# Four gated levels as products with only the second halves' queries, in a RetNet and HGRN2 step on one core

## The chip, the core and the metric

The kernel runs on one NeuronCore of a Trainium2 chip. Its time is the device time of one execution in microseconds (us), the median of several runs. TensorE (PE in the profile) multiplies matrices. It first loads a stationary operand (LDWEIGHTS, listed as the engine PEld) and then streams a moving operand past it (MATMUL). VectorE (DVE), ScalarE (ACT) and GpSimd (POOL) work element by element on 128 partitions. SyncE (SP) issues the DMA transfers. Products land in PSUM, everything else lies in SBUF.

## The reference, cut to what matters

One decoder layer is run for a prompt of 2048 tokens and for eight samples of 8 tokens each. After a norm and one input projection there are four RetNet heads and four HGRN2 heads. The change is in the HGRN2 heads, which are a linear recurrence with a forget gate of its own for every feature:

```
b = jnp.cumsum(gb, axis=2)
diff = b[:, :, :, None, :] - b[:, :, None, :, :]
decay = jnp.exp(jnp.where(causal[:, :, None], diff, -jnp.inf))
A = jnp.einsum('bhtd,bhsd,bhtsd->bhts', qb, kb, decay)
o = jnp.einsum('bhts,bhsv->bhtv', A, vb) + jnp.einsum('bhtd,bhdv->bhtv', qb * jnp.exp(b), S)
```

`A[t, s]` is needed for all pairs s <= t within a chunk. Its decay depends on the feature d, so it is not one product of queries and keys. A head norm, a gate, the output projection and a squared-ReLU MLP follow.

## The kernel before

Tokens are worked on in three groups of 640, 768 and 704 (the last with the 64 sample tokens ahead of 640 of the prompt). For each group `mix` runs four heads, and one call of `mixer` does a RetNet and an HGRN2 head together on chunks of 128 tokens. A group has 5, 6 and 5 chunks, in two segments: 2 and 3, 3 and 3, 2 and 3. So there are 12 calls of `mixer`, with 64 chunks in all. After the mixing come the output projection and the MLP (`ffn`) of the three groups, which the change does not touch.

Projections are written as three float32r products each (high part by high part, high by low, low by high). They are the matmuls of L344, L751 and L1212, and they fill PE. The work of a head is laid between them: `mixer` enters its steps into an agenda at given ticks, a tick being one step of a projection (six matmuls), and a scheduler then orders each engine's instructions.

The matrix `A` of a chunk (tile `AT`, transposed: keys by queries; `ATs` for the samples) is put together from levels. On the level of w in `LEVELS = (64, 32, 16, 8, 4, 2)` a chunk falls into blocks of 2w tokens, and the pairs are those with the key in the first half of a block and the query in its second half. `exponents`, `decays` and `decayed` make a tile `qk` that holds decayed keys in first halves and decayed queries in second halves, so that the features can be summed by a product.

- For w = 64 and 32 `corners` (L978) multiplies each first half by its second half: 64 by 64 or 32 by 32 columns.
- For w = 16, 8 and 4 `kept` (L921, for the samples L915) multiplies the whole chunk by itself, 128 by 128 columns in float32, and `copy_predicated` (L922, L916) copies the entries of this level's mask `msk[:, i]` into `AT`.
- For w = 2, blocks of four tokens, `quad_products` (L989) forms the four products of a block's two keys and two queries feature by feature on DVE, `quad_parts` cuts them into two float32r parts (ACT L351, DVE L352), and `quad` sums over features by `column_sums`, two matmuls with a matrix of ones as stationary operand (L512, L513). Copies of 64 elements (L1010, L1008) place the four results.
- Neighbours (w = 1) and the diagonal have steps of their own, also with `column_sums`.

A float32 matmul is listed as two passes, each with its own LDWEIGHTS. `mm` gives PSUM tiles out of four buffers, and `pj` is a pool of two for the projections. A projection's result leaves PSUM by `normed` (DVE L650). Where a row names L853, these are the transposes of `turn`; L784 and L787 are the sample outputs, L798 the cutting of sample values, L1069 the decayed keys of the chunk's end.

Of the kernel before, what the change touches and what calls it, by code (L numbers as in the profile page):

```python
# [13 lines left out]
ALU = mybir.AluOpType  # L14

P = 128
# [4 lines left out]
SLEN = 8  # L21
NS = NSEQ * SLEN
# [11 lines left out]
LEVELS = (64, 32, 16, 8, 4, 2)  # L34
NLV = len(LEVELS) + 2
# [67 lines left out]
def in_groups(sample, prompt):  # L103

    out = []
    for ns, p0, n in GROUPS:
        out += [sample[:ns], prompt[p0:p0 + n]]
    return np.concatenate(out, 0)


def constants():
    c = np.zeros((P, NCONST), np.float64)
    c[:, C_ID:C_ID + P] = np.eye(P)
    s = np.arange(P)[:, None]
    t = np.arange(P)[None, :]
    sc = DK ** -0.5
    same = (s // SLEN == t // SLEN) & (s < NS) & (t < NS)
    for h, g in enumerate(GAM):
        dec = np.where(s <= t, g ** np.maximum(t - s, 0), 0.0) * sc
        c[:, C_RM + h * P:C_RM + (h + 1) * P] = dec  # L120
        c[:, C_RS + h * P:C_RS + (h + 1) * P] = np.where(same, dec, 0.0)
        c[:, C_GQ + h * P:C_GQ + (h + 1) * P] = g ** (t + 1.0)
        c[:, C_GS + h * NS:C_GS + (h + 1) * NS] = g ** (np.arange(NS) % SLEN + 1.0)
        c[:, C_KS + h] = sc * g ** (P - 1.0 - s[:, 0])
        c[:, C_KSS + h] = sc * g ** (SLEN - 1.0 - s[:, 0] % SLEN)
    c[:, C_SM:C_SM + 4] = (s % 32 // SLEN == np.arange(4)[None, :])
    m = np.zeros((P, 2 * NLV, P), np.float32)
    for i, w in enumerate(LEVELS + (1,)):
        lv = (s // (2 * w) == t // (2 * w)) & (s % (2 * w) < w) & (t % (2 * w) >= w)
        m[:, i] = lv  # L130
        m[:, NLV + i] = lv & (s < NS) & (t < NS) & (w < SLEN)

    i = LEVELS.index(2)
    m[:, 0], m[:, NLV] = m[:, i] * (s % 2), m[:, NLV + i] * (s % 2)
    m[:, NLV - 1] = s == t
    m[:, 2 * NLV - 1] = (s == t) & (s < NS)
    half = DK // 2
    inv = np.power(10000.0, (-np.arange(half, dtype=np.float32) / np.float32(half)).astype(np.float64)).astype(np.float32)
    pos = in_groups(np.tile(PAST + np.arange(SLEN), NSEQ), np.arange(SEQ)).astype(np.float32)
    ang = (inv[:, None] * pos[None, :]).astype(np.float64)  # L140
    cs = np.zeros((P, 2, NT), np.float32)
    cs[:half, 0] = cs[half:, 0] = np.cos(ang)
    cs[:half, 1] = -np.sin(ang)
    cs[half:, 1] = np.sin(ang)
    return c.astype(np.float32), m.astype(np.uint8).reshape(P, -1), cs.reshape(P, -1)
# [57 lines left out]
class Kernel:  # L203
# [5 lines left out]
    def at(self, when, fn, *a):  # L209
        heapq.heappush(self.agenda, (when, self.n_at, fn, a))  # L210
        self.n_at += 1
# [651 lines left out]
    def mixer(self, g, p, b, t0):  # L863


        nc, T, n0 = self.nc, g.T, g.ns
        con, msk = self.con, self.msk
        n = g.n // C
        q, k, f = b["q"], b["k"], b["f"]
        rq, rk = b["rq"], b["rk"]  # L870
        cols = [slice(n0 + C * c, n0 + C * (c + 1)) for c in range(n)]
        x = {}
        at = lambda t, fn, *a: self.at(t0 + t, fn, *a)
# [15 lines left out]
        def blocks(t, w, a):  # L889
            return t[:, a:T].rearrange("p (n h m) -> p n h m", h=2, m=w)  # L890
# [13 lines left out]
        def decayed(w):  # L904
            a = 0 if w < SLEN else n0
            qk = x["qk", w] = self.get()
            D4, Q4 = blocks(x["dd", w], w, a), blocks(qk, w, a)
            nc.vector.tensor_tensor(out=Q4[:, :, 0, :], in0=D4[:, :, 0, :], in1=blocks(k, w, a)[:, :, 0, :], op=ALU.mult)
            nc.vector.tensor_tensor(out=Q4[:, :, 1, :], in0=D4[:, :, 1, :], in1=blocks(q, w, a)[:, :, 1, :], op=ALU.mult)

        def kept(i, qk, sg):

            if sg == 2:
                ps = self.mm(P)
                nc.tensor.matmul(ps, qk[:, :P], qk[:, :P], start=True, stop=True)  # L915
                nc.vector.copy_predicated(self.ATs, msk[:, NLV + i], ps)  # L916
                return
            seg, m = g.segs[sg], len(g.segs[sg])
            ps = self.mm(m * P)
            for j, c in enumerate(seg):  # L920
                nc.tensor.matmul(ps[:, j * P:(j + 1) * P], qk[:, cols[c]], qk[:, cols[c]], start=True, stop=True)  # L921
            nc.vector.copy_predicated(self.AT[sg][:, :m], msk[:, i].unsqueeze(1).to_broadcast([P, m, P]),  # L922
                                      ps.rearrange("p (c t) -> p c t", t=P))


        def own_products():
# [42 lines left out]
        def corners(w, sg):  # L969

            nb = P // (2 * w)
            seg, m = g.segs[sg], len(g.segs[sg])
            qk = x["qk", w]
            ps = self.mm(m * nb * w)
            for j, c in enumerate(seg):
                for r in range(nb):
                    s0 = cols[c].start + 2 * w * r
                    nc.tensor.matmul(ps[0:w, (r * m + j) * w:(r * m + j + 1) * w], qk[:, s0:s0 + w], qk[:, s0 + w:s0 + 2 * w],  # L978
                                     start=True, stop=True)
            for r in range(nb):  # L980
                nc.scalar.copy(self.AT[sg][2 * w * r:2 * w * r + w, :m, 2 * w * r + w:2 * w * (r + 1)],
                               ps[0:w, r * m * w:(r + 1) * m * w].rearrange("p (c t) -> p c t", t=w))


        def quad_products():
            x["quad"] = self.get()
            Q4 = x["qk", 2][:, :T].rearrange("p (n h m) -> p n h m", h=2, m=2)
            shape = [P, T // 4, 2, 2]
            nc.vector.tensor_tensor(out=x["quad"][:, :T].rearrange("p (n i j) -> p n i j", i=2, j=2),  # L989
                                    in0=Q4[:, :, 1].unsqueeze(3).to_broadcast(shape),  # L990
                                    in1=Q4[:, :, 0].unsqueeze(2).to_broadcast(shape), op=ALU.mult)

        def quad_parts():
            x["quad_hi"], x["quad_lo"] = self.getr(), self.getr()
            self.cut(x["quad"], x["quad_hi"], x["quad_lo"], T, 3)

        def quad(sg):
            seg, m = g.segs[sg], len(g.segs[sg])
            a, e = self.seg_cols(g, seg)
            s0 = cols[seg[0]].start  # L1000
            second = lambda t: t.rearrange("p (n h i) -> p n h i", h=2, i=2)[:, :, 1]
            ps = self.mm(e - a)
            self.column_sums(ps, x["quad_hi"][:, a:e], x["quad_lo"][:, a:e])
            p4 = ps.rearrange("p (n i j) -> p n i j", i=2, j=2)
            nb, nq = (s0 - a) // 4, P // 4
            for j, i in ((0, LEVELS.index(2)), (1, 0)):
                if nb:
                    nc.vector.copy_predicated(second(self.ATs[:, :NS]), second(msk[:, NLV + i, :NS]), p4[:, :nb, :, j])  # L1008
                for c in range(m):
                    nc.vector.copy_predicated(second(self.AT[sg][:, c]), second(msk[:, i]),  # L1010
                                              p4[:, nb + c * nq:nb + (c + 1) * nq, :, j])

        def level(i, sg):
            w = LEVELS[i]
            if w == 2:
                quad(sg)
            elif w >= 32:
                corners(w, sg)
            else:
                kept(i, x["qk", w], sg)  # L1020
# [99 lines left out]
            x["gate", i, hd] = self.gate_norm(g, x["po", i][hd], a, e, b["gh" if hd else "gr"], self.eps_h if hd else self.eps, g.o[p][hd])  # L1120

        parts = range(3 if n0 else 2)
        step, late, chunk, wait = 13, 24, 7, 14
        at(0, logs)
        at(4, scans)
        at(40, own_products)
# [7 lines left out]
        for i, w in enumerate(LEVELS):  # L1134
            t = 6 + step * i
            at(t, exponents, w)
            at(t + 8, decays, w)
            at(t + 11, decayed, w)
            if w == 2:
                at(t + 16, quad_products)  # L1140
                at(t + 20, quad_parts)
            for sg in (parts if 2 < w < SLEN else range(2)):
                at(t + late + 3 * sg + (wait if w == 2 else 9 if w >= 32 else 4), level, i, sg)
        for sg in parts:
            at(46 + 4 * sg, ret_scores, sg)
            at(60 + 4 * sg, turn, "ktr", rk, sg, C_KS)
# [1 line left out]
        t = 6 + step * len(LEVELS)  # L1148
# [680 lines left out]
```

## Time and profile before

| | us |
|---|---|
| median of 3 runs (2497.9 to 2498.38) | 2497.9 |
| the profiled execution | 2499.3 |
| its span, first to last instruction | 2497.5 |
| PE busy, share of the span | 2483.4 (99%) |
| PEld busy | 2465.2 (99%) |
| DVE busy | 1883.1 (75%) |
| ACT busy | 1246.5 (50%) |
| POOL busy | 371.2 (15%) |

The profiled execution is 1.4 us longer than the median. PE and PEld overlap: the load of one matmul's stationary operand runs while the matmul before it still streams. A MATMUL's record is longer than its share of the engine, since matmuls are pipelined; what one costs is read from how far apart the records start.

### The profile page before, as it was taken

To read this page: it belongs to the slowest core of one execution; us is meant where nothing else is said; L and a number is where in the kernel's file an instruction comes from. 1 tells how busy PE (TensorE), PEld (TensorE's weight loads), DVE (VectorE), ACT (ScalarE), POOL (GpSimd) and SP (SyncE) were. 2 spreads that over 40 slices of the span, in tenths; PEclk is the share of its full clock that TensorE was granted. 3 is DMA by queue.
4 is the path that set the end of the run, shared out by engine and by line. 5 is a ranking of instruction groups with operands and counts; after the bars stand their busy time and mean duration, and the time that the engine had idled before them with its cause. 6 is when DMAs were issued, how large, how long until landed. Compare 5 with 4: busy or idle time off the path is not lost.

```text
span 2497.5 us, 41452 instructions
## 1 busy us (share of the span) xinstructions
PE 2483.4 (99%) x16536; PEld 2465.2 (99%) x16536; DVE 1883.1 (75%) x2453; ACT 1246.5 (50%) x1674; POOL 371.2 (15%) x312
## 2 busy tenths in 40 slices
PE   9999999999999999999999999999999999999998
PEld 9999999999999999999999999999999999999998
DVE  7666866667685766686875899776699878778987
ACT  6665653444464444453644554544454436445544
POOL 5223304324411442340000000000000000000000
PEclk9999999999999999999999999999999999999999
DMA  7454575465566665868866856576675545867552
GB/s 264 170 183 172 206 252 180 161 228 186 189 205 244 216 217 197 265 210 257 283 222 214 284 196 214 176 237 222 201 264 177 188 151 192 282 195 246 195 188 89
DMA packets 191655, 525.67 MB, mean 210 GB/s; under 512 B 20963, under 2 KB 62435, under 8 KB 191462
## 3 DMA queue, kind: packets, MB, share of 16 engines
q1 hardware_dynamic: 191318, 523.01, 61.9%
q8 instruction: 130, 2.13, 0.3%
q14 instruction: 63, 0.52, 0.1%
q10 hardware_dynamic: 144, 0.02, 0.0%
HBM read 389.51 MB, written 132.39 MB: 209 GB/s over the span
## 4 chain that ended last, share of the span: by engine, by line
PE 97%; DVE 1%; ACT 1%; DMA 0%; issue 0%; SPq 0%; DVEq 0%; ACTq 0%
PE pj L344 29%; PE pf L1212 26%; PE pj L1212 25%; PE pjv L751 8%; PE mm L921 2%; PE po L1101 1%; PE mm L1109 1%; PE po L1103 1%; PE mm L978 1%; PE mm L513 1%; PE mm L512 1%; PE mm L1035 1%; PE mm L853 1%; PE po L787 1%; DMA slab<-x 0%
## 5 line engine op out<-in xcount | busy, mean ns | idle before, releaser
L273 ACT CAST hi<-raw 128x1024 fp32r<-128x1024 f32 x392 | 411.8, 1050 | 612.7 <-PE pf L1212 258.0
L344 PE MATMUL pj<-slab,hi 128*128 128x320 f32 (+2 forms) x3072 | 660.7, 328 | 2.9 <-DVE slab L650 1.3
L1212 PE MATMUL pf<-slab,hi 128*128 128x320 f32 (+2 forms) x2768 | 658.4, 321 | 0.0
L1212 PE MATMUL pj<-slab,hi 128*128 128x352 f32 (+2 forms) x2608 | 621.3, 322 | 0.0
L287 DVE TENSOR_TENSOR lo<-raw,hi 128x1024 fp32r<-128x1024 f32 x392 | 486.2, 1241 | 113.2 <-ACT hi L273 107.8
L344 PEld LDWEIGHTS pj<-slab,hi 128*128 128x128 f32 x3072 | 508.2, 188 | 5.7 <-DVE slab L650 1.6
L1212 PEld LDWEIGHTS pf<-slab,hi 128*128 128x128 f32 x2768 | 481.2, 188 | 0.0
L1212 PEld LDWEIGHTS pj<-slab,hi 128*128 128x128 f32 x2608 | 453.7, 188 | 0.1
L1212 PE MATMUL pf<-slab,lo 128*128 128x320 f32 (+2 forms) x1384 | 444.7, 321 | 0.0
L1212 PE MATMUL pj<-slab,lo 128*128 128x352 f32 (+2 forms) x1304 | 419.5, 322 | 0.0
L344 PE MATMUL pj<-slab,lo 128*128 128x320 f32 (+2 forms) x1536 | 379.0, 328 | 0.6 <-DVE lo L287 0.6
L344 PEld LDWEIGHTS pj<-slab,lo 128*128 128x128 f32 x1536 | 263.3, 188 | 1.5 <-DVE lo L287 1.1
L1212 PEld LDWEIGHTS pf<-slab,lo 128*128 128x128 f32 x1384 | 259.6, 188 | 0.0
L1212 PEld LDWEIGHTS pj<-slab,lo 128*128 128x128 f32 x1304 | 244.6, 188 | 0.0
L751 PE MATMUL pjv<-hi,slab 128*128 128x256 f32 (+1 forms) x1056 | 199.4, 285 | 0.0
L1303 ACT CAST slab<-slab 128x640 fp32r<-128x640 f32 (+2 forms) x192 | 145.4, 778 | 64.2 <-DVE slab L1314 51.7
L1307 DVE TENSOR_TENSOR slab<-slab 128x640 fp32r<-128x640 f32 (+2 forms) x192 | 167.3, 887 | 8.5 <-PE pj L1212 2.8
L751 PEld LDWEIGHTS pjv<-hi,slab 128*128 128x128 f32 (+1 forms) x1056 | 166.3, 190 | 1.4
L751 PE MATMUL pjv<-lo,slab 128*128 128x256 f32 (+1 forms) x528 | 149.2, 283 | 0.0
L902 ACT ACTIVATE slab<-slab 128x640 f32<-128x640 f32 (+2 forms) x72 | 56.3, 782 | 154.2 <-POOL slab L898 154.0
L751 PEld LDWEIGHTS pjv<-lo,slab 128*128 128x128 f32 (+1 forms) x528 | 100.3, 190 | 0.0
L1557 DVE TENSOR_TENSOR slab<-pf,slab 128x640 f32<-128x640 f32 (+2 forms) x88 | 77.7, 888 | 29.5 <-PE pf L1212 29.1
(222 smaller groups left out, 3012.4 us busy)
## 6 DMA issues: line engine op xcount, KB each, us to landing
raw<-w SPq DMA_DIRECT2D x264, 512.0 KB, 4.2
slab<-u SPq DMA_DIRECT2D x32, 384.0 KB, 4.6
u<-ld SPq DMA_DIRECT2D x30, 384.0 KB, 4.5
slab<-u SPq DMA_DIRECT2D x32, 352.0 KB, 4.5
u<-ld SPq DMA_DIRECT2D x30, 352.0 KB, 3.7
slab<-u SPq DMA_DIRECT2D x32, 320.0 KB, 5.0
u<-ld SPq DMA_DIRECT2D x30, 320.0 KB, 4.0
ld<-x SPq DMA_DIRECT2D x16, 384.0 KB, 3.8
```

The costliest lines, as they stand in the source:

```text
L273: self.nc.scalar.copy(hi, raw)
L287: self.nc.vector.tensor_tensor(out=lo, in0=self.second.pop(j), in1=hi.bitcast(F32), op=ALU.subtract)
L344: self.nc.tensor.matmul(pj[:, i, :T2], w, a[:, c0:c1], start=j == 0 and q == 0, stop=j == n - 1 and q == 2)
L512: self.nc.tensor.matmul(ps, self.ones_r, hi, start=True, stop=False)
L513: self.nc.tensor.matmul(ps, self.ones_r, lo, start=False, stop=True)
L751: nc.tensor.matmul(pj[:m, i * 256:(i + 1) * 256], a[:, s:s + m], ww, start=kb == 0 and q == 0, stop=m == C and kb == KB - 1 and q == 2, sk ...
L902: nc.scalar.activation(x["dd", w][:, a:T], x["dd", w][:, a:T], AF.Exp)
L921: nc.tensor.matmul(ps[:, j * P:(j + 1) * P], qk[:, cols[c]], qk[:, cols[c]], start=True, stop=True)
L1212: self.nc.tensor.matmul(*a, **k)
L1303: self.nc.scalar.copy(hi[:, :g.T], B[name][:, :g.T])
L1307: self.nc.vector.tensor_tensor(out=lo[:, :g.T], in0=B[name][:, :g.T], in1=hi.bitcast(F32)[:, :g.T], op=ALU.subtract)
L1557: nc.vector.tensor_tensor(out=r, in0=ps, in1=r, op=ALU.add)
```

## The change

`kept` now uses as moving operand only the second halves of the blocks, which are the queries: 64 columns for each chunk and 32 for the samples, every second run of w columns. The stationary operand stays the whole chunk of 128 columns. The product's PSUM tile is half as wide, and `copy_predicated` copies its 64 columns a chunk into the second halves of `AT`, under the same half of the mask. The level of w = 2 takes this path too; `quad_products`, `quad_parts`, `quad` and the masks made for them go. So this level has one more float32 matmul for each chunk, and in the last group one more for the samples, in place of two column sums for each segment. It comes ten ticks earlier in the agenda.

```diff
         def kept(i, qk, sg):
 
+            w = LEVELS[i]
+            second = lambda t: t.rearrange("p (n h m) -> p n h m", h=2, m=w)[:, :, 1]
             if sg == 2:
-                ps = self.mm(P)
-                nc.tensor.matmul(ps, qk[:, :P], qk[:, :P], start=True, stop=True)
-                nc.vector.copy_predicated(self.ATs, msk[:, NLV + i], ps)
+                ps = self.mm(NS // 2).rearrange("p (n m) -> p n m", m=w)
+                nc.tensor.matmul(ps, qk[:, :P], second(qk[:, :NS]), start=True, stop=True)
+                nc.vector.copy_predicated(second(self.ATs[:, :NS]), second(msk[:, NLV + i, :NS]), ps)
                 return
             seg, m = g.segs[sg], len(g.segs[sg])
-            ps = self.mm(m * P)
+            ps = self.mm(m * P // 2).rearrange("p (c n m) -> p c n m", c=m, m=w)
             for j, c in enumerate(seg):
-                nc.tensor.matmul(ps[:, j * P:(j + 1) * P], qk[:, cols[c]], qk[:, cols[c]], start=True, stop=True)
-            nc.vector.copy_predicated(self.AT[sg][:, :m], msk[:, i].unsqueeze(1).to_broadcast([P, m, P]),
-                                      ps.rearrange("p (c t) -> p c t", t=P))
+                nc.tensor.matmul(ps[:, j], qk[:, cols[c]], second(qk[:, cols[c]]), start=True, stop=True)
+            nc.vector.copy_predicated(self.AT[sg][:, :m].rearrange("p c (n h m) -> p c n h m", h=2, m=w)[:, :, :, 1],
+                                      second(msk[:, i]).unsqueeze(1).to_broadcast([P, m, P // (2 * w), w]), ps)
...
-        def quad_products():
...
-        def quad_parts():
...
-        def quad(sg):
...
         def level(i, sg):
             w = LEVELS[i]
-            if w == 2:
-                quad(sg)
-            elif w >= 32:
+            if w >= 32:
                 corners(w, sg)
             else:
                 kept(i, x["qk", w], sg)
...
-            if w == 2:
-                at(t + 16, quad_products)
-                at(t + 20, quad_parts)
-            for sg in (parts if 2 < w < SLEN else range(2)):
-                at(t + late + 3 * sg + (wait if w == 2 else 9 if w >= 32 else 4), level, i, sg)
+            for sg in (parts if w < SLEN else range(2)):
+                at(t + late + 3 * sg + (9 if w >= 32 else 4), level, i, sg)
```

On PE, in the first head of the first group, what followed the level of w = 4 before were the column sums of `quad` (L512, L513), between the projections of L344 and beside the transposes of L853:

```order
L344 MATMUL pj<-slab,hi 128x320 x4
L344 MATMUL pj<-slab,lo 128x320 x2
L512 MATMUL mm<-slab,ones_r 128x256
L513 MATMUL mm<-slab,ones_r 128x256
L344 MATMUL pj<-slab,hi 128x320 x4
L853 MATMUL mm<-con,slab 128x128 x2
L344 MATMUL pj<-slab,lo 128x320 x2
L512 MATMUL mm<-slab,ones_r 128x384
L513 MATMUL mm<-slab,ones_r 128x384
```

In the changed kernel (line numbers are its own: L341 is the projection, L920 `kept`) the same stretch of the first head is:

```order
L341 MATMUL pj<-slab,hi 128x320 x4
L920 MATMUL mm<-slab 128x64 x2
L341 MATMUL pj<-slab,lo 128x320 x2
L341 MATMUL pj<-slab,hi 128x320 x4
L920 MATMUL mm<-slab 128x64 x3
L341 MATMUL pj<-slab,lo 128x320 x2
```

Two and three float32 matmuls of 64 moving columns stand where four column sums stood, 20 projection matmuls earlier.

On DVE, in the last head of the last group, this stood before between the last copies of the level of w = 4 and the copies of `quad` (L650 takes a projection out of PSUM):

```order
L989 TENSOR_TENSOR slab<-slab 128x704
L922 COPY_PREDICATED AT_174<-msk,mm 128x384
L916 COPY_PREDICATED ATs<-msk,mm 128x128
L1069 TENSOR_TENSOR slab<-slab 128x704
L352 TENSOR_TENSOR slab<-slab 128x704
L798 TENSOR_TENSOR slab<-ld,slab 32x256 x2
L1244 TENSOR_TENSOR raw<-raw 128x1024
L650 TENSOR_TENSOR slab<-pj,slab 128x704
```

In the changed kernel (L921 and L915 are the copies of `kept`, L795 the sample values, L1209 sums of weights, L1037 the decayed keys, L647 the projection's way out) it is:

```order
L921 COPY_PREDICATED AT_174<-msk,mm 128x48x4
L915 COPY_PREDICATED ATs<-msk,mm 128x8x4
L795 TENSOR_TENSOR slab<-ld,slab 32x256 x2
L1209 TENSOR_TENSOR raw<-raw 128x1024
L1037 TENSOR_TENSOR slab<-slab 128x704
L647 TENSOR_TENSOR slab<-pj,slab 128x704
L921 COPY_PREDICATED AT_173<-msk,mm 128x64x2
L921 COPY_PREDICATED AT_174<-msk,mm 128x96x2
```

The products and the cut of `quad` (L989 and the L352 behind L1069) are gone from ahead of the projection's way out, the decayed keys now stand behind the sample values, and the copies of w = 2 stand behind the projection's way out.

## Rows read from the trace of the kernel before

**Rows 1.** The page: the span, and busy time by engine.

```profile
span 2497.5 us, 41452 instructions
PE 2483.4 (99%) x16536; PEld 2465.2 (99%) x16536; DVE 1883.1 (75%) x2453; ACT 1246.5 (50%) x1674; POOL 371.2 (15%) x312
```

**Rows 2.** Busy time by stretch (mixing, then the rest), with the granted clock (PEclk).

```profile
0.00:1165.00 1165.00, 1160.11 (x8272) 1143.33 (x8273) 817.71 (x1277) 597.70 (x908) 371.22 (x312) 1.00 0.61 211
1165.00:2497.50 1332.50, 1323.32 (x8266) 1321.88 (x8264) 1065.35 (x1177) 648.78 (x767) 0.00 (x0) 1.00 0.64 210
```

**Rows 3.** Timeline of PE around a `kept` of three chunks: start, length, count.

```profile
68.93 0.45 PE L344 MATMUL pj<-slab,lo 128*128 128x320 f32 x2
69.22 0.83 PE L921 MATMUL mm<-slab 128*128 128x128 f32 x6
69.80 0.83 PE L344 MATMUL pj<-slab,hi 128*128 128x320 f32 x4
70.47 0.46 PE L344 MATMUL pj<-slab,lo 128*128 128x320 f32 x2
70.77 0.75 PE L344 MATMUL pj<-slab,hi 128*128 128x320 f32 x4
71.35 0.46 PE L344 MATMUL pj<-slab,lo 128*128 128x320 f32 x2
```

**Rows 4.** Timeline of PE at the column sums of `quad`, same head.

```profile
80.68 0.28 PE L512 MATMUL mm<-slab,ones_r 128*128 128x256 f32 x1
80.79 0.28 PE L513 MATMUL mm<-slab,ones_r 128*128 128x256 f32 x1
80.91 0.75 PE L344 MATMUL pj<-slab,hi 128*128 128x320 f32 x4
...
82.01 0.34 PE L512 MATMUL mm<-slab,ones_r 128*128 128x384 f32 x1
82.18 0.33 PE L513 MATMUL mm<-slab,ones_r 128*128 128x384 f32 x1
82.35 0.75 PE L344 MATMUL pj<-slab,hi 128*128 128x320 f32 x4
```

**Rows 5.** Loads by form: stationary operand (rows*columns), count, busy us, mean ns.

```profile
L921 PEld LDWEIGHTS mm<-slab 128*128 128x128 f32 x384 | 51.9, 191 | 0.1
...
L978 PEld LDWEIGHTS mm<-slab 128*32 128x32 f32 x256 | 9.9, 112 | 5.3 <-issue 3.5 <-PE mm L1027 0.9 <-ACT slab L351 0.6
L978 PEld LDWEIGHTS mm<-slab 128*64 128x64 f32 x128 | 9.2, 137 | 3.4 <-issue 0.8
```

**Rows 6.** Timeline of PE, last head of the last group: the wait there.

```profile
1123.33 0.91 PE L344 MATMUL pj<-slab,hi 128*128 128x352 f32 x4 [1.32 <-DVE slab L650]
```

**Rows 7.** Timeline of DVE ahead of that wait.

```profile
1115.88 0.89 DVE L989 TENSOR_TENSOR slab<-slab 128x704 f32<-128x704 f32 x1
...
1118.15 0.89 DVE L352 TENSOR_TENSOR slab<-slab 128x704 fp32r<-128x704 f32 x1
1119.07 2.15 DVE L798 TENSOR_TENSOR slab<-ld,slab 32x256 fp32r<-32x256 f32 x2
1121.25 1.23 DVE L1244 TENSOR_TENSOR raw<-raw 128x1024 f32<-128x1024 f32 x1
1122.39 0.89 DVE L650 TENSOR_TENSOR slab<-pj,slab 128x704 f32<-128x704 f32 x1
```

**Rows 8.** Timeline of PE around `corners` of 64 by 64.

```profile
497.18 0.28 PE L751 MATMUL pjv<-hi,slab 128*128 128x256 f32 x1
497.39 0.56 PE L978 MATMUL mm<-slab 128*64 128x64 f32 x6
497.88 0.39 PE L751 MATMUL pjv<-hi,slab 128*128 128x256 f32 x1
498.10 0.28 PE L751 MATMUL pjv<-lo,slab 128*128 128x256 f32 x1
498.22 0.40 PE L751 MATMUL pjv<-hi,slab 128*128 128x256 f32 x2
498.46 0.28 PE L751 MATMUL pjv<-lo,slab 128*128 128x256 f32 x1
```

More of the change, by code (lines that the diff above doesn't have):

```diff
@@ L131, in constants @@
         m[:, NLV + i] = lv & (s < NS) & (t < NS) & (w < SLEN)
-    i = LEVELS.index(2)
-    m[:, 0], m[:, NLV] = m[:, i] * (s % 2), m[:, NLV + i] * (s % 2)
     m[:, NLV - 1] = s == t
@@ L982, in corners @@
                                ps[0:w, r * m * w:(r + 1) * m * w].rearrange("p (c t) -> p c t", t=w))
-        def quad_products():
[L986 to L991, printed above, removed]
-        def quad_parts():
-            x["quad_hi"], x["quad_lo"] = self.getr(), self.getr()
-            self.cut(x["quad"], x["quad_hi"], x["quad_lo"], T, 3)
-        def quad(sg):
[L998 to L1011, printed above, removed]
         def level(i, sg):
             w = LEVELS[i]
-            if w == 2:
-                quad(sg)
-            elif w >= 32:
+            if w >= 32:
                 corners(w, sg)
@@ L1122, in mixer @@
         parts = range(3 if n0 else 2)
-        step, late, chunk, wait = 13, 24, 7, 14
+        step, late, chunk = 13, 24, 7
         at(0, logs)
```

## Prediction, made before the changed kernel ran

> **What bounds the kernel now.** I read the page's busy times first, then the busy time by stretch, then PE's timeline, where single insertions between the projections can be priced, then the loads by form, and DVE only at the place where PE waits for it.
>
> PE is busy for 99% of the span [rows 1], for 1160.11 of the 1165.00 us of mixing and 1323.32 of the 1332.50 us of the rest [rows 2]. The granted clock is 1.00 in both stretches, the upper level of 2.4 GHz. DVE and ACT have slack as a whole. So the time is nearly the sum of what PE's matmuls cost, and the change is priced by what it adds to and takes from that stream. Idle time matters only where another engine keeps PE waiting.
>
> **What a pass costs.** A record of an inserted matmul says little by its length, since it overlaps its neighbours, so I measure an insertion by how far it moves the projections. In the stream of projections of 320 columns, six matmuls (one "lo x2" row to the next without anything between) take 71.35 - 70.47 = 0.88 us [rows 3]. With a `kept` of three chunks between, "lo x2" to "lo x2" takes 70.47 - 68.93 = 1.54 us, so the insertion costs 0.66 us. That is six passes (two for each float32 matmul) of 0.111 us.
>
> Each pass has two sides that run beside those of its neighbours: the load of 128 stationary columns and the stream of 128 moving columns. The change halves the stream alone: `second()` is applied to the moving operand, and the stationary one stays `qk[:, cols[c]]`, 128 columns. What it brings depends on which side sets the pace. The loads' records give the load's own side: 112 ns for 32 columns, 137 for 64, 191 for 128 [rows 5]. From 64 to 128 columns it grows by 54 ns, 0.84 ns a column; 128 columns therefore take about 108 ns of loading, the rest of a record being latency that the next load overlaps. So the load by itself accounts for nearly the whole 111 ns of a pass. Halving the stream to about 55 ns leaves a pass waiting for the next load. I expect passes of 0.108 to 0.111 us in the changed `kept`, and take 0.1095.
>
> The Trainium skill ("TensorE: Matmul & The Clock Gate", section "LDWEIGHTS (loading the stationary operand)") says that a load takes the number of stationary columns over 1.2 ns, whatever the contraction; that would be 107 ns for 128 columns, beside the 108 ns worked out above. The same page (section "Step-by-step: what each phase is for", on the fill) says that throughput is purely the number of moving columns in cycles; by that alone the passes would halve, which is the first rival below.
>
> **The sum on PE.** All counts are for 12 heads and 64 chunks.
> - Passes before: three levels by 64 chunks by two, and in the last group four heads by one sample product by two: 384 + 8 = 392. At 0.111 us that is 43.5 us.
> - Passes after: four levels by 64 by two, and two sample levels: 512 + 16 = 528. At 0.1095 us that is 57.8 us. A sample product keeps 128 stationary columns, so it is a pass like any other.
> - Removed column sums: two matmuls for a segment. The pair of 256 columns costs 80.91 - 80.68 = 0.23 us, the pair of 384 costs 82.35 - 82.01 = 0.34 us [rows 4]. The last group's first segment has 320 columns (64 of the samples and 256), which I put between, at 0.29. There are 4 pairs of 256, 16 of 384 and 4 of 320: 0.9 + 5.4 + 1.2 = 7.5 us.
> - Together 57.8 - 43.5 - 7.5 = **+6.8 us**. With passes at 0.108 it is +6.0, at 0.111 +7.6.
>
> This is the core of the argument: the old level of w = 2 was cheap on PE, 7.5 us, because its stationary operand of ones took few loads for many columns; as products it takes 128 more chunk passes and 8 more for the samples, about 15 us. The narrower stream gives nothing back for them.
>
> **What goes from the other engines.** For each head DVE loses the product (0.89 us [rows 7]), the cut (0.89 us) and 10 to 12 small copies; ACT loses one cast. The remaining copies get half as wide, and two or three are added for w = 2. None of this is on the path as long as PE is busy, so I cost it at nothing, with one exception. In the last head PE waits 1.32 us for L650, which takes a projection out of PSUM [rows 6]. Ahead of L650 on DVE stand the product L989 and the cut L352 of `quad`, 1.78 us together, then L798, L1244 and L650 itself, with hardly a gap [rows 7]. Without the two, L650 comes up to 1.78 us earlier and the wait could go. Against that, the new copies of w = 2 stand behind L650 on DVE, and the transposes of the decayed keys, which need the PSUM tiles that those copies free, now wait for them. So I take **-1.0 us**, between -1.7 and +1.
>
> Does the product of w = 2 itself make PE wait? It stands 20 projection matmuls, some 2.9 us, behind the last `kept` of w = 4, and needs `decayed(2)` from DVE, which is where the level of w = 4 has its own; no such wait is seen there in any head, so I cost it at nothing. If that cover failed once in each head by 0.2 us it would be 2.4 us. Reading the moving operand in runs of two to sixteen columns is shown by no row; the stream has some 50 ns of slack beside the load, so up to twice the time for it costs nothing. Its bound from above is a stream at 111 ns again, the +7.6 above. Fewer small tiles on DVE and ACT cannot lengthen the MLP stretch, and the order of the weights' transfers stays as it is.
>
> Sum: +6.8 - 1.0 = +5.8 us. Against the profiled execution's 2499.3 us this is 2505.1; against the median of 2497.9, **2503.7 us**, +0.23%. That is just above 0.2% (5.0 us), which is about what a measurement of this kernel can tell from no change. The forecast's own range, with passes from 0.108 to 0.111 us and the wait from -1.7 to +1, is +4.3 to +8.6, 2502.2 to 2506.5 us.
>
> **The rivals.**
> 1. *The stream sets the pace, not the load.* Then each pass falls to about half, 0.056 us, and the sample passes to about 0.03: 512 x 0.056 + 16 x 0.03 = 29.2, minus 43.5 and 7.5: -21.8 us, **2476 us**, faster by 0.9%. It decides as soon as a pass of 64 moving columns against 128 stationary ones takes less than 0.097 us, since 528 x 0.097 = 51.0 is the price at which the sum is zero. For it: at 128 by 128 both sides take about the same, so the rows cannot say which one is waited for. Against it: the load's growth by columns [rows 5]. Chance 5%.
> 2. *The waits pay for the passes.* The wait of 1.3 us goes, shorter ones of the heads before with it, passes run at the bare 0.108, and the transitions gain a little: +6.0 - 2.5 = +3.5 us, or less, **2501 us**, within 0.2%. For it: PE's idle time in mixing is 1165.00 - 1160.11 = 4.9 us [rows 2], part of it at the start. Chance 36%.
> 3. *A narrow stream breaks the pipeline.* `corners` of 64 by 64 do: from 497.18 to 498.22 us lie three projections of 0.12 us (498.46 - 498.22 for two) and six narrow passes [rows 8], so the passes cost 1.04 - 0.36 = 0.68 us, where half of 0.111 for each would be 0.33. Some 0.35 us are paid for entering and leaving. If 64 moving columns alone did this, the 8 insertions a head and 8 for the samples, 104 in all, would cost 36 us more: **2540 us**. Against it: there the stationary operand is narrow too, and only that changes which part of the array is loaded. Chance 4%.
> 4. *The transposes wait.* The copies behind L647 hold the PSUM tiles in more heads than the last, 1 us in the four heads of the last group: +6.8 + 4 = +10.8, **2508.7 us**. Chance 6%.
>
> The forecast has 49%. It lies near the bound of 0.2%, so I give a tenth of its chance to "no change": faster 5%, within 0.2% 41%, slower 54%. The range that leaves out rivals 1 and 3 and the ends of the others is 2500.0 to 2507.0 us.
>
> **What would show it.** Right: the loads of `kept` still some 190 ns, and a `kept` of three chunks moving the projections by 0.65 us, although its matmuls stream half the columns; PE's matmul count up by 136 - 48 = 88; no column sums behind the level of w = 4; the wait for L647 in the last head shorter. Wrong: an insertion of three chunks at 0.35 us (rival 1) or near 1 us (rival 3), or a new wait of PE for the copies of `kept`.

## The result, and the profile after

The changed kernel takes 2502.24 us (median of 22 runs, 2501.18 to 2503.95) against 2497.9 us for the kernel before (22 runs, 2497.21 to 2499.61). The ratio is 1.0016, with a 95% interval of 1.001 to 1.0022. So it is slower by 4.3 us, just inside the 0.2% that I called no change. The forecast was 2503.7 us, within 2500.0 to 2507.0.

The head of the page after, which answers to [rows 1]:

```profile
span 2500.2 us, 41537 instructions
PE 2487.7 (100%) x16624; PEld 2470.5 (99%) x16624; DVE 1846.1 (74%) x2321; ACT 1240.2 (50%) x1662; POOL 378.7 (15%) x312
```

PE has the 88 matmul records more that the counts gave (16624 - 16536). DVE is busy 37 us less. By itself that buys no time, since it counts only where PE waits for DVE.

The next two rows show where the time went. Each lists the matmuls of the MLP that write `pf`, with their first and last start; the first is of the kernel before, the second of the changed one.

```profile
L1212 PE MATMUL pf<-slab,hi x2768: 307/322/346, 1192.9 to 2486.1; 128*128 128x320 f32 x69, 128*128 128x384 f32 x65, 128*128 128x352 f32 x64
```

```profile
L1177 PE MATMUL pf<-slab,hi x2768: 302/322/346, 1197.2 to 2488.9; 128*128 128x320 f32 x69, 128*128 128x384 f32 x65, 128*128 128x352 f32 x64
```

The MLP starts 1197.2 - 1192.9 = 4.3 us later. That is the whole difference of the medians. By the last of these matmuls the gap is 2.8 us, since the two profiled executions differ in the MLP as well; the last section shows that this lies in the MLP's own pace.

PE's timeline after, in the same head as [rows 3]:

```profile
68.89 0.46 PE L341 MATMUL pj<-slab,lo 128*128 128x320 f32 x2
69.19 0.78 PE L920 MATMUL mm<-slab 128*128 128x64 f32 x6
69.77 0.82 PE L341 MATMUL pj<-slab,hi 128*128 128x320 f32 x4
70.43 0.46 PE L341 MATMUL pj<-slab,lo 128*128 128x320 f32 x2
70.73 0.75 PE L341 MATMUL pj<-slab,hi 128*128 128x320 f32 x4
71.31 0.46 PE L341 MATMUL pj<-slab,lo 128*128 128x320 f32 x2
```

From "lo x2" to "lo x2" it is 70.43 - 68.89 = 1.54 us with the product between and 71.31 - 70.43 = 0.88 us without. The product costs 0.66 us, as before, although it streams 64 columns and not 128. Its record is shorter (0.78 us, before 0.83), which would mislead whoever reads lengths.

The loads of the changed kernel by form, which answer to [rows 5]:

```profile
L920 PEld LDWEIGHTS mm<-slab 128*128 128x128 f32 x512 | 69.2, 191 | 0.1
...
L914 PEld LDWEIGHTS mm<-slab 128*128 128x128 f32 x16 | 2.8, 189 | 0.0
```

The loads are unchanged, 191 ns each (189 for the samples), and there are 528 of them where there were 392.

What PE waited for after, in us in total, times, longest:

```profile
PE mm L408 <- DVE eps L412: 1.1, 1, 1.1
PE pj L341 <- DVE slab L1237: 0.8, 1, 0.8
PE pf L1721 <- ACT slab L1712: 0.7, 1, 0.7
PE pj L341 <- ACT hi L270: 0.6, 1, 0.6
```

The wait of [rows 6] for the projection's way out is gone. DVE's timeline in the last head, beside [rows 7]:

```profile
1121.62 1.77 DVE L795 TENSOR_TENSOR slab<-ld,slab 32x256 fp32r<-32x256 f32 x2
1123.43 1.22 DVE L1209 TENSOR_TENSOR raw<-raw 128x1024 f32<-128x1024 f32 x1
1124.57 0.88 DVE L1037 TENSOR_TENSOR slab<-slab 128x704 f32<-128x704 f32 x1
1125.37 0.88 DVE L647 TENSOR_TENSOR slab<-pj,slab 128x704 f32<-128x704 f32 x1
```

PE at the place where it waited before:

```profile
1127.46 0.49 PE L850 MATMUL mm<-con,slab 128*128 128x128 f32 x3
1127.70 0.57 PE L341 MATMUL pj<-slab,hi 128*128 128x352 f32 x2
```

Product and cut no longer stand ahead of L647, and the copies there are shorter. Counted from the same projection matmul (1114.48 us before, 1120.11 after), PE reaches this place after 7.5 us before and 7.6 after, so it comes hardly later. But L650 ended after 8.8 us, and L647 ends after 6.1. What went is DVE's lateness.

### The profile page after: what moved, and what is told of

Read it like the earlier page. It is cut to its first block, busy times and chain, and to the rows that moved or that the text cites. A ratio compares the mean times of both kernels' runs of the same rounds, so it can differ in the third digit from the quotient of the medians.

```text
span 2500.2 us, 41537 instructions
## 1 busy us (share of the span) xinstructions
PE 2487.7 (100%) x16624; PEld 2470.5 (99%) x16624; DVE 1846.1 (74%) x2321; ACT 1240.2 (50%) x1662; POOL 378.7 (15%) x312
## 4 chain that ended last, share of the span: by engine, by line
PE 98%; DVE 1%; ACT 0%; DMA 0%; SPq 0%; DVEq 0%; issue 0%
PE pj L341 30%; PE pf L1177 26%; PE pj L1177 25%; PE pjv L748 8%; PE mm L920 2%; PE po L1069 1%; PE mm L1077 1%; PE po L1071 1%; PE mm L977 1%; PE mm L1003 1%; PE po L784 1%; PE mm L510 1%; PE mm L509 1%; PE mm L850 1%; DMA slab<-x 0%; ACT slab L546 0%
## 5 line engine op out<-in xcount | busy, mean ns | idle before, releaser
L341 PE MATMUL pj<-slab,hi 128*128 128x320 f32 (+2 forms) x3072 | 661.9, 329 | 1.7 <-DVE slab L1237 0.8
L341 PEld LDWEIGHTS pj<-slab,hi 128*128 128x128 f32 x3072 | 506.6, 188 | 4.5 <-DVE slab L1237 1.0
L341 PE MATMUL pj<-slab,lo 128*128 128x320 f32 (+2 forms) x1536 | 379.7, 328 | 0.6 <-DVE lo L284 0.6
L341 PEld LDWEIGHTS pj<-slab,lo 128*128 128x128 f32 x1536 | 263.1, 188 | 1.4 <-DVE lo L284 1.1
```

The lines of the kernel that those rows point to most:

```text
L341: self.nc.tensor.matmul(pj[:, i, :T2], w, a[:, c0:c1], start=j == 0 and q == 0, stop=j == n - 1 and q == 2)
```

## The experiments

The theory: the load of the stationary operand sets the pace of a pass, so the narrow stream gives nothing, and the change costs what the new products of w = 2 cost beyond the column sums that they replace. The first rival: the stream does count, and something else eats its gain. The second: a narrow stream breaks the pipeline. In what follows "the MLP's start" is the first start of the rows above, 1192.9 us before.

**Narrow products alone.** On the kernel before, `kept` becomes that of the changed kernel, and the level of w = 2 stays as it was:

```diff
-            ps = self.mm(m * P)
+            ps = self.mm(m * P // 2).rearrange("p (c n m) -> p c n m", c=m, m=w)
             for j, c in enumerate(seg):
-                nc.tensor.matmul(ps[:, j * P:(j + 1) * P], qk[:, cols[c]], qk[:, cols[c]], start=True, stop=True)
+                nc.tensor.matmul(ps[:, j], qk[:, cols[c]], second(qk[:, cols[c]]), start=True, stop=True)
...
             if w == 2:
                 quad(sg)
```

> The narrow products with second halves' queries for the levels of w = 16, 8 and 4 alone; the level of w = 2 stays feature by feature with its column sums. If the load of 128 stationary columns sets the pace of a pass, the 392 passes keep their 0.111 us and nothing is gained but some 0.05 us at each of 12 places where a narrow product stands right ahead of transposes: 2497.4 us, between 2496.5 and 2498.5, with the wait for the projection's way out in the last head still there. If the stream set the pace, the passes would cost half: about -20 us, 2478 us. If it is the narrower copies on DVE that matter, the wait of 1.3 us in the last head goes: 2496 us.

It took 2496.16 us against 2497.43 us (ratio 0.9994, 0.9985 to 1.0003). The passes did not get cheaper, so the stream does not set the pace: a product of three chunks still moves the projections by 0.67 us. The time is that of the third expectation, but the wait for L650 of which it spoke only shrank, from 1.3 to 1.0 us. The gain, if it is one, is small, and the interval does not exclude that there is none. What the trace shows of it is 0.05 us at each place with transposes right behind, and shorter delays in the last group; but the profiled execution is the fastest of the eleven (2494.61 us), so it may show more than the median has. The first expectation was 1.2 us too high, and the time lies 0.3 us below its range.

**The whole chunk streamed again,** with the level of w = 2 as products:

```diff
-            ps = self.mm(m * P // 2).rearrange("p (c n m) -> p c n m", c=m, m=w)
+            ps = self.mm(m * P)
             for j, c in enumerate(seg):
-                nc.tensor.matmul(ps[:, j], qk[:, cols[c]], second(qk[:, cols[c]]), start=True, stop=True)
+                nc.tensor.matmul(ps[:, j * P:(j + 1) * P], qk[:, cols[c]], qk[:, cols[c]], start=True, stop=True)
+            ps = ps.rearrange("p (c n h m) -> p c n h m", c=m, h=2, m=w)[:, :, :, 1]
```

> The changed kernel with the whole chunk streamed again (128 columns, for the samples too) on all four levels; only the copies take the second halves. If the load sets the pace this costs next to nothing: 2502.7 us, between 2502 and 2503.5, a product of three chunks moving the projections by 0.67 us as in the changed kernel. If the narrow stream saves anything, the 528 passes cost up to 0.05 us more each: up to 2528 us.

It took 2503.55 us against 2497.43 (ratio 1.0026, 1.0016 to 1.0036). That is 6.1 us above the kernel before, where the changed kernel is 4.3 above. Doubling the stream of 528 passes thus costs under 2 us: 0.6 of them where transposes follow, and most of the rest is one delay of 0.9 us at a sample output in the last head (read from the slowest of the eight executions, which is the profiled one). Twice the stream costs next to nothing in the passes themselves.

**Four widths of the stream in one kernel,** by level:

```diff
+            n = {16: 128, 8: 96, 4: 64, 2: 32}[w]
...
+                nc.tensor.matmul(ps[:, j * n:(j + 1) * n], qk[:, cols[c]], qk[:, cols[c]][:, :n], start=True, stop=True)
```

> The changed kernel with 128, 96, 64 and 32 moving columns (the first of each chunk) on the levels of w = 16, 8, 4 and 2, always against 128 stationary ones. It leaves out the products with the other queries of a chunk. A product of three chunks (six passes): 0.67 us at every width if the load sets the pace; 0.67, 0.50, 0.33 and 0.17 if the stream does; above 0.67 at 32 if a narrow stream breaks the pipeline as the products of 64 by 64 seem to.

One execution took 2503.09 us. A product of three chunks moved the projections by 0.67 us at 128, 96, 64 and 32 columns (medians 0.670, 0.670, 0.671, 0.669). PE's timeline at 32 columns:

```profile
77.67 0.75 PE L341 MATMUL pj<-slab,hi 128*128 128x320 f32 x4
78.26 0.75 PE L921 MATMUL mm<-slab 128*128 128x32 f32 x6
78.84 0.54 PE L341 MATMUL pj<-slab,lo 128*128 128x320 f32 x2
79.22 0.75 PE L341 MATMUL pj<-slab,hi 128*128 128x320 f32 x4
```

It is 79.22 - 77.67 = 1.55 us from "hi x4" to "hi x4" and 0.88 without, so 0.67 us for the six passes, with a quarter of the columns streamed. This also ends the rival that a narrow stream breaks the pipeline.

**Four widths of the load in one kernel,** the stream always 64 columns:

```diff
+            k = {16: 128, 8: 112, 4: 96, 2: 64}[w]
...
-                nc.tensor.matmul(ps[:, j], qk[:, cols[c]], second(qk[:, cols[c]]), start=True, stop=True)
+                nc.tensor.matmul(ps[:k, j], qk[:, cols[c]][:, :k], second(qk[:, cols[c]]), start=True, stop=True)
```

> The changed kernel with 128, 112, 96 and 64 stationary columns (the first keys of each chunk) on the levels of w = 16, 8, 4 and 2, the stream being 64 columns throughout. It leaves out the products with the other keys. If the load sets the pace, at 0.84 ns a column and some 3 ns: six passes cost 0.67, 0.58 and 0.50 us, and at 64 columns 0.35 us, or 0.69 if a narrow stationary operand is what costs the 0.34 us of entering and leaving that the products of 64 by 64 show. If a pass has a fixed price instead, 0.67 at every width.

One execution took 2501.05 us. The loads by form (those of 128 columns take 190 ns), and PE's timeline around 96 and then 64 stationary columns:

```profile
L921 PEld LDWEIGHTS mm<-slab 128*112 128x112 f32 x128 | 15.9, 177 | 0.0
L921 PEld LDWEIGHTS mm<-slab 128*96 128x96 f32 x128 | 14.4, 164 | 0.1
L921 PEld LDWEIGHTS mm<-slab 128*64 128x64 f32 x128 | 9.2, 135 | 5.4 <-issue 5.1 <-DVE slab L1038 0.2
```

```profile
73.02 0.45 PE L341 MATMUL pj<-slab,lo 128*128 128x320 f32 x2
73.31 0.45 PE L341 MATMUL pj<-slab,hi 128*128 128x320 f32 x2
73.60 0.64 PE L921 MATMUL mm<-slab 128*96 128x64 f32 x6
74.05 0.54 PE L341 MATMUL pj<-slab,hi 128*128 128x320 f32 x2
74.43 0.45 PE L341 MATMUL pj<-slab,lo 128*128 128x320 f32 x2
...
77.92 0.75 PE L341 MATMUL pj<-slab,hi 128*128 128x320 f32 x4
78.60 0.56 PE L921 MATMUL mm<-slab 128*64 128x64 f32 x6
79.09 0.56 PE L341 MATMUL pj<-slab,lo 128*128 128x320 f32 x2
79.49 0.75 PE L341 MATMUL pj<-slab,hi 128*128 128x320 f32 x4
```

At 96 columns the product costs 1.41 - 0.88 = 0.53 us, at 64 columns 1.57 - 0.88 = 0.69. The medians are 0.671, 0.603, 0.536 and 0.693 us. I had expected 0.58 and 0.50 at 112 and 96. The difference says which load counts: not a pass's own but the one behind it. (By their own loads, six passes at 96 columns would cost 0.51 us.) Of six passes five have a short load behind them, and the last has a projection's load of 128 columns. At 96 columns that is 5 x 0.085 + 0.111 = 0.536 us, where 0.085 is 96 x 0.84 ns and 4 ns, the 4 ns being what a pass of 0.112 us has over a load of 0.108. At 112 it is 5 x 0.098 + 0.111 = 0.602. So, summed over a product, a pass costs the longer of its own stream and the next matmul's load. At 64 columns that would be 5 x 0.058 + 0.111 = 0.40 us, and 0.29 us come on top: a stationary operand of 64 columns is what makes PE stop on entering and leaving, as in [rows 8], and 96 columns do not.

**Without the level of w = 2,** on the kernel before:

```diff
-            if w == 2:
-                at(t + 16, quad_products)
-                at(t + 20, quad_parts)
-            for sg in (parts if 2 < w < SLEN else range(2)):
+            for sg in (() if w == 2 else parts if w < SLEN else range(2)):
```

> The kernel before without the level of w = 2 altogether: no products, cut, column sums or copies for it; it leaves out the pairs of key and query within blocks of four tokens. This tells what the level cost before: on PE its 24 pairs of column sums, 7.9 us by how far they move the projections. If the waits of the last group's heads (2.5 us in all) come from the work that this level gives to DVE and ACT, they go as well: about 2487.2 us. If they come from something else, 2489.6 us and the wait for the projection's way out still stands in the last head.

It took 2487.93 us against 2497.57 (ratio 0.9962, 0.9948 to 0.9975), and the MLP starts at 1183.1 us, 9.8 earlier. The column sums are 7.9 of it (medians 0.36, 0.29 and 0.24 us for a pair of 384, 320 and 256 columns). Some 0.6 us are a quicker start of this execution: its projections are ahead by that much at 52 us, before any work of this level. The other 1.4 us are waits, net: those for L650 and in the other heads of the last group go, and a new one comes, of PE for the decayed keys of the chunk's end:

```profile
PE mm L853 <- DVE slab L1069: 0.8, 1, 0.8
```

So with the level PE waits longer, by some 2.2 us before the new wait is taken off.

**Fewer copies.** Narrow products on three levels, and the copies of `quad` merged over the chunks of a segment:

```diff
-                for c in range(m):
-                    nc.vector.copy_predicated(second(self.AT[sg][:, c]), second(msk[:, i]),
-                                              p4[:, nb + c * nq:nb + (c + 1) * nq, :, j])
+                nc.vector.copy_predicated(self.AT[sg][:, :m].rearrange("p c (n h i) -> p c n h i", h=2, i=2)[:, :, :, 1],
+                                          second(msk[:, i]).unsqueeze(1).to_broadcast([P, m, nq, 2]),
+                                          p4[:, nb:, :, j].rearrange("p (c n) i -> p c n i", c=m))
```

> The narrow products on w = 16, 8 and 4, the level of w = 2 by column sums as before, its 10 to 12 small copies in a head merged to 4 to 6. PE's stream is that of the run with narrow products alone (2496.2 us). If DVE's queue ahead of the projection's way out is what makes PE wait in the last head, the wait of 1.3 us there shrinks only by what the copies ahead of it weigh, some 0.3 us, since most of them stand behind it: 2496 us, between 2495 and 2497. If it shrinks wholly, 2495 us.

It took 2495.61 us against 2497.57 (ratio 0.9992, 0.9983 to 1.0001). The wait for L650 stays at 1.0 us. The copies stand behind L650, and their number is not what PE waits for.

**Short loads.** This follows from the run with four widths of the load: `corners` becomes one product of 96 by 64 columns for each chunk, and `kept` loads only the columns up to the last key.

```diff
+            k = P - w
...
-                nc.tensor.matmul(ps[:, j], qk[:, cols[c]], second(qk[:, cols[c]]), start=True, stop=True)
+                nc.tensor.matmul(ps[:, j], qk[:, cols[c]][:, :k], second(qk[:, cols[c]]), start=True, stop=True)
...
-                for r in range(nb):
-                    s0 = cols[c].start + 2 * w * r
-                    nc.tensor.matmul(ps[0:w, (r * m + j) * w:(r * m + j + 1) * w], qk[:, s0:s0 + w], qk[:, s0 + w:s0 + 2 * w],
-                                     start=True, stop=True)
+                nc.tensor.matmul(ps[:96, j], qk[:, cols[c]][:, :96],
+                                 qk[:, cols[c]].rearrange("p (n h m) -> p n h m", h=2, m=w)[:, :, 1], start=True, stop=True)
```

> As the run with merged copies, and every product of a gated level loads only the keys that it needs: 112, 120 and 124 stationary columns for w = 16, 8 and 4, and for w = 64 and 32 one product of 96 stationary by 64 moving columns for each chunk in place of the products of 64 by 64 and 32 by 32. If a pass costs what the load behind it takes, 0.844 ns a column and 4 ns, and 96 columns pay nothing for entering and leaving, the levels of 64 and 32 cost 0.54 and 0.37 us (three and two chunks) in place of 0.69 and 0.57, together -8.2 us, and the others give -2.4 us: 2485.5 us, between 2484.5 and 2487. If one matmul for each chunk costs the same as before whatever its load, the levels of 64 and 32 go to 0.67 and 0.45: 2493.5 us.

It took 2486.92 us against 2497.57 (ratio 0.9958, 0.9946 to 0.9971). The levels of 64 and 32 now cost 0.53 and 0.37 us a product, as expected, and the levels of 16, 8 and 4 cost 0.60, 0.64 and 0.65 us for three chunks, which is what the rule of the next load gives for 112, 120 and 124 columns. The gain is 10.7 us, and the time 1.4 us above the expected 2485.5. PE's timeline at the level of 64, to be read beside [rows 8]:

```profile
493.19 0.28 PE L751 MATMUL pjv<-hi,slab 128*128 128x256 f32 x1
493.31 0.64 PE L979 MATMUL mm<-slab 128*96 128x64 f32 x6
493.76 0.36 PE L751 MATMUL pjv<-hi,slab 128*128 128x256 f32 x1
493.96 0.28 PE L751 MATMUL pjv<-lo,slab 128*128 128x256 f32 x1
494.08 0.40 PE L751 MATMUL pjv<-hi,slab 128*128 128x256 f32 x2
```

The product starts 0.12 us after the projection ahead of it, the ordinary pace, where in [rows 8] it was 0.21. From that projection to the third behind it are 494.08 - 493.19 = 0.89 us; less three projections of 0.12 the product costs 0.53, where it was 0.68. Part of the missing 1.4 us is a new wait of 1.3 us in the first head, where the products of 32 need a PSUM tile that DVE gives back late (L979 for L1037).

**Transposes between.** A RetNet key's transpose stands behind each product of w = 16:

```diff
                 nc.tensor.matmul(ps[:, j], qk[:, cols[c]][:, :k], second(qk[:, cols[c]]), start=True, stop=True)
+                if beside is not None:
+                    nc.tensor.transpose(beside[:, j * P:(j + 1) * P], rk[:, cols[c]], self.ident)
```

> As the run with short loads, and the transposes of the RetNet keys stand between the chunk products of w = 16, one behind each, instead of in groups of two and three. If a pass costs what the load behind it takes, the second pass of each of 64 products now costs some 0.065 us in place of 0.098 or 0.111, since a transpose's load is short: about -2 us against the run with short loads, 2483.5 us. If only the load's own size counts, no difference; if the mixing of transposes and products breaks the pipeline, slower.

It took 2485.42 us against 2497.57 (ratio 0.9953, 0.9939 to 0.9966): 1.5 us better than without, where some 2 were expected. PE's timeline:

```profile
63.31 0.32 PE L924 MATMUL mm<-slab 128*112 128x64 f32 x2
63.47 0.28 PE L926 MATMUL mm<-con,slab 128*128 128x128 f32 x1
63.58 0.32 PE L924 MATMUL mm<-slab 128*112 128x64 f32 x2
```

A product of two passes takes 63.47 - 63.31 = 0.16 us and a transpose 0.11. The first pass waits for the second's load (0.098), the second only for the transpose's, so it costs some 0.065. That is less than the 0.098 of its own load, which once more shows that the load behind counts.

**The product of w = 2 on GpSimd:**

```diff
-            nc.vector.tensor_tensor(out=x["quad"][:, :T].rearrange("p (n i j) -> p n i j", i=2, j=2),
+            nc.gpsimd.tensor_tensor(out=x["quad"][:, :T].rearrange("p (n i j) -> p n i j", i=2, j=2),
...
-                at(t + 16, quad_products)
+                at(t + 14, quad_products)
```

> As the run with short loads and transposes between, and the product of the level of w = 2 is made by GpSimd, two ticks earlier, instead of VectorE. If the 1.3 us wait for the projection's way out in the last head comes from the 0.9 us of product and 0.9 us of cut that stand ahead of it on VectorE, it shrinks by about 0.9 us and the time is 2484.5 us. If GpSimd, which works beside it at longer instructions, brings the product too late, the column sums or their transposes wait in more heads: 2486 us or more.

It took 2491.19 us against 2497.18 (ratio 0.9975, 0.9966 to 0.9984), some 6 us worse than with the product on DVE. On GpSimd the product takes 2.2 us for 704 tokens, on DVE 0.89. The wait for L650 stayed (1.2 us), and PE waited in more heads, for copies into `AT` and for the states that stand behind them:

```profile
PE pj L344 <- DVE slab L650: 1.2, 1, 1.2
...
PE po L1113 <- DVE S L1126: 0.8, 1, 0.8
...
PE po L784 <- DVE AT L1012: 0.4, 1, 0.4
```

The expectation of a shorter wait missed, and the timelines of the last head show why. The first row is from the run with the product on DVE, the other two are from this one:

```profile
1102.43 1.68 DVE L352 TENSOR_TENSOR slab<-slab 128x704 fp32r<-128x704 f32 x2
```

```profile
1106.03 2.58 DVE L352 TENSOR_TENSOR slab<-slab 128x704 fp32r<-128x704 f32 x2
1104.80 2.27 POOL L992 TENSOR_TENSOR slab<-slab 128x704 f32<-128x704 f32 x1 [3.54 <-DVE slab L909]
```

While GpSimd makes the product, the two cuts on DVE, of which the first runs beside it, take 2.58 us in place of 1.68. So DVE loses there the 0.9 us that it was to gain, and L650 comes no earlier.

## Why the prediction was right, and where it was off

- **PE is the bound, and the stream of matmuls is to be priced.** Right. The 4.3 us lie before the MLP, and the two medians differ by as much.
- **The load sets the pace of a pass, the stream does not.** Right, and shown from both sides: four stream widths at 0.67 us, four load widths at four prices. The term was still sized a little low: I took 0.1095 us for a pass, and it is 0.1117 (0.670 / 6).
- **The sum on PE, +6.8 us.** After: 64 products of three chunks at 0.670, 32 of two at 0.445, 8 of the samples at 0.224 are 58.9 us. At 12 places a transpose's short load follows the product, which saves 0.045 to 0.053 us each, 0.6 us; this I had not seen. Before it was 43.7 us, and the column sums were 7.9 (I had 7.5). 58.9 - 0.6 - 43.7 - 7.9 = +6.7 us. So the sum came out, but in part by luck: the passes were priced 1.1 us too low, and the transposes, the passes before and the column sums make up for it.
- **The waits, -1.0 us.** This is the term of the sum that was mis-sized: 4.3 - 6.7 = -2.4 us, outside the -1.7 to +1 that I had given. The wait of 1.3 us for L650 went wholly. I had set against it that the transposes might now wait for copies behind L647; they do not: the first of them start at 1126.28 us with no idle time ahead of them, while the first of those copies, begun at 1126.17, still runs. The rest are delays that I had not priced. In the kernel before, the second of two column sums in the last head (L513) starts at 1119.10 us, 0.42 behind the first, where 0.15 is the ordinary pace; it needs the second half of the cut, which DVE ends at 1119.04. And two sample outputs of the last group start 0.2 and 0.3 us later than their like in other heads. After, such delays are a few tenths in all. For the wait for L650 it is shown that this level's work on DVE and ACT was the cause: it goes in the run without the level, and with narrow products alone 1.0 us of it stays. For the small delays it is not: they are gone as well in the profile of the narrow products alone, which keeps this work and only has lighter copies on DVE.
- **Rival 2,** that the waits pay for the passes, had 2501 us, and the measurement lies between it (1.2 us away) and the forecast (1.5 us away). Its 2.5 us of waits were about right, its passes of 0.108 us were not. So the forecast had the better price of a pass, and the rival the better price of the waits. The case that I thought likeliest, slower by over 0.2%, was missed by 0.7 us. Rival 1 (2476 us) and rival 3 (2540 us) are refuted by the run with four stream widths; rival 4 (waits of the transposes) did not occur.

## What to carry to other kernels

Before a moving operand is made narrower, look at what is loaded behind it: a short matmul costs the load of the next one, and here, in float32 against 128 stationary columns, 32 to 128 streamed columns cost the same. What pays is fewer stationary columns (down to 96 without loss, while 64 made PE stop on entering and leaving), or a matmul with a short load right behind a short stream; the two together, with the column sums kept for w = 2, gave a kernel of 2485.42 us, 0.47% faster than the one before. A way of computing that keeps one stationary operand for many columns, as the sums by ones did (7.9 us for w = 2), can beat one that looks leaner but loads for each block (16 x 0.670 + 8 x 0.445 + 4 x 0.224 = 15.2 us). And moving work from DVE to GpSimd can slow down what DVE does beside it.

## What was not expected of the hardware

- A float32 transpose loads faster than a float32 product: 141 ns for 128 columns where products take 191, as this row of the kernel before shows, so, as an estimate with the same latency in both, about 58 ns of loading where a product has 108.

```profile
L853 PEld LDWEIGHTS mm<-con,slab x128: 137/141/144, 62.2 to 1121.6; 128*128 128x128 f32 x128
```

- In the third group's MLP the same projections of 352 columns run at two paces. The kernel before, then the changed one, over about the same stretch of work:

```profile
2101.00:2214.00 113.00, 113.00 (x703) 113.00 (x702) 83.23 (x96) 57.44 (x70) 0.00 (x0) 1.00 0.75 248
```

```profile
2105.00:2217.00 112.00, 112.00 (x707) 112.00 (x706) 83.44 (x97) 57.57 (x70) 0.00 (x0) 1.00 0.75 251
```

The granted clock is 1.00 in both, yet it is 0.161 us for a matmul in the first and 0.158 in the second. From the first to the last of these 2688 matmuls all eleven profiles show one of two lengths, about 431.2 or 429.6 us, with no relation that I can see to what a kernel does in the mixing: the kernel before and the run with whole chunks streamed have the long one, the changed kernel and the fastest one the short. That is 1.5 of the 1.6 us by which the two profiled spans differ less than the medians. The fastest and the slowest run of the kernel before lie 2.4 us apart. What switches the pace, and whether it makes that spread, was not tried.
